# Head norms of a DeltaNet block through one shared root and a spreading product

## The chip, the cores and the metric

The kernel runs on one core of a Trainium2 chip. The metric is the device time of one execution in microseconds (us); lower is better. The engines are named as the profile names them: PE is TensorE (PEld its weight loads), ACT is ScalarE, DVE is VectorE, POOL is GpSimd and SP is SyncE, whose queue (SPq) issues the transfers.

## The reference

One decoder block, float32, 512 positions, width 1024. Its input projection feeds two token mixers, a gated DeltaNet and an RWKV-7 mixer, which are merged, projected, and followed by a ConvGLU. The change touches the start of the DeltaNet, which has 8 heads of 64 channels:

```python
def l2_normalize(x, eps=1e-6):
    return x * lax.rsqrt(jnp.sum(x * x, axis=-1, keepdims=True) + eps)

q = l2_normalize(heads(q)) * (GDN_HEAD_DIM ** -0.5)
k = l2_normalize(heads(k))
g = -jnp.exp(a_log) * jax.nn.softplus(a_logit + dt_bias)
...
diff = g_cum[..., :, None] - g_cum[..., None, :]
decay = jnp.where(causal, jnp.exp(jnp.where(causal, diff, 0.0)), 0.0)
lower = jnp.where(strict, einsum('bhncd,bhnsd->bhncs', k_beta, k) * decay, 0.0)
attn = jnp.where(causal, einsum('bhncd,bhnsd->bhncs', q, k) * decay, 0.0)
```

So each position's 64 channels of a head are divided by the root of their sum of squares (q and k), decay factors are made from the running sums of g in chunks of 64 positions, and the scores of k with k and of q with k are multiplied by them. A triangular solve per chunk and head follows.

## The kernel before

Activations lie with channels on the 128 partitions and the 512 positions along the free dimension. The DeltaNet's k and q are `kq[:, a, j]`, with a = 0 for k and a = 1 for q, and j = 0 to 3: eight tiles of 128x512, each holding two heads.

**The stream.** The large products (projections, FFN) are done in three TensorE products per 128 rows (`mm3`, lines 186, 189 and 190): the upper part of the weights by the upper part of the data, by its lower part, and the lower part of the weights by the upper part of the data. Weights come from memory to `raw` (line 156, issued by SP), and ACT casts them to `whi` (line 145), and DVE subtracts (line 148, `wlo`); each of these has two buffers. `fill(n)` puts n such steps of three products into the instruction stream between other work. The products of a tile of 128 outputs (8 steps, 24 products) go to a bank of `ps_mm`, of which there are two; the bank is read by ACT and DVE (lines 392, 394, 398, 399), or copied to `tmp_sp` and stored (lines 404, 405). The stream's tiles at this place in the program are, in order: one whose output is called LO1, then LO2, four Z tiles (stored by line 405) and four GV tiles.

**The norms.** `l2norm` (lines 486 to 493) is called eight times with two fills behind each: ACT squares the tile (line 488), PE multiplies by `ones_bd`, a block matrix of ones that puts each head's sum on all 64 of its partitions (line 490, an fp32 product 128*128 by 128x512 into a bank of `ps_pa`), ACT takes the logarithm and the exponential of minus a half of it (`rstd_of`, both recorded at line 94, output `tmp_rs`), and DVE multiplies (line 493).

**The decay parts.** A loop over b = 0 to 3 (lines 508 to 528) has one DVE product (line 510, `tmp_acc`), an fp32 product with `tri_gt` (line 514), an exponential on ACT into `tmp_sg`, two masks on POOL (line 519), a DVE product (line 521), then an fp32 product with `ones_x` (line 525), which sums over the 64 partitions of the other half, and an exponential into `eg`.

**The scores.** A loop over eight chunks (lines 627 to 635) has eight products of 64*64 by 64x128 (line 631) into one of three `ps_pa` banks, which DVE reads in three products (lines 632, 635, 635). A DVE product of 64x2048 (line 626) stands ahead of them in DVE's order. `solve` follows: SP writes the scores to memory in four transfers (line 556) and reads them back (line 559), then DVE runs a recursion of 30 steps (lines 567, 569).

**What sets the order.** The code is written in one order; a scheduler then sets each engine's instructions in a row of its own, and every engine works through its row in order. `ps_pa` has three banks, `ps_pc` has three, and `tmp_sq`, `tmp_rs`, `tmp_acc`, `tmp_sg` and `tmp_sp` have two buffers each.

Of the kernel before, what the change touches and what calls it, by code (L numbers as in the profile page):

```python
# [17 lines left out]
AF = mybir.ActivationFunctionType  # L18
ALU = mybir.AluOpType
# [23 lines left out]
CONS = {}  # L43
_n = 0
for _name, _w in (("ident", 128), ("tri_gt", 128), ("cumtri", 128),
                  ("ones_x", 128), ("mask2", 128), ("tri_le", 64), ("sel", 16)):
    CONS[_name] = (_n, _w)
    _n += _w
NCONS = _n
# [6 lines left out]
def body(ctx, tc, io, out, tap=lambda name, ap: None):  # L56
    nc = tc.nc
    pe, act, dve, pool, sp = nc.tensor, nc.scalar, nc.vector, nc.gpsimd, nc.sync
# [19 lines left out]
    pa = lambda: bank("pa", 3)  # L78
    pc = lambda: bank("pc", 3)
# [21 lines left out]
    def tmp(tag, bufs=2):  # L101
        return tp.tile([128, 512], F32, name=f"tmp_{tag}", tag=tag, bufs=bufs)
# [18 lines left out]
    def con(name):  # L121
        o, w = CONS[name]
        return cons[:, o:o + w]

    ident, tri_gt, cumtri = (con(n) for n in ("ident", "tri_gt", "cumtri"))
    mask2 = con("mask2").rearrange("p (a t) -> p a t", a=2)
    tri_le, sel, ones_x = con("tri_le"), con("sel"), con("ones_x")
    kc = const.tile([128, 4], F32, name="kc")
    for j, v in enumerate((EPS, LNX)):
        pool.memset(kc[:, j:j + 1], v)  # L130
# [143 lines left out]
    def fill(n=1):  # L274
        for _ in range(n):
            if gen[0] is None:
                if not queue:
                    return
                gen[0] = stream()
            try:  # L280
                next(gen[0])
            except StopIteration:
                gen[0] = None
# [10 lines left out]
    def rstd_of(p, scale, dst, bias=eps):  # L294
        fn(dst, p, AF.Ln, bias=bias, scale=scale)
        return fn(dst, dst, AF.Exp, scale=-0.5)
# [54 lines left out]
    p = pa()  # L351
# [131 lines left out]
    last["gate"] = dve.scalar_tensor_tensor(gl, s3, -1.0, bc(nea), op0=ALU.mult, op1=ALU.mult)  # L483


    def l2norm(dst, scale):
        sq = tmp("sq")
        act.activation(sq, dst, AF.Square)
        q = pa()
        pe.matmul(q, ones_bd, sq, start=True, stop=True)  # L490
        rs = tmp("rs")
        rstd_of(q, 1.0, rs)
        dve.scalar_tensor_tensor(dst, dst, scale, rs, op0=ALU.mult, op1=ALU.mult)

    eg = ct4(slot(3))
    ee = slot2(1)[:, 0:2048].rearrange("p (c h t) -> p c h t", c=NC, h=4)
    for j in range(4):
        l2norm(kq[:, 0, j], 1.0)
        fill(2)
        l2norm(kq[:, 1, j], 0.125)  # L500
        fill(2)
    p = pa()
    kdec = const.tile([128, NC, 4], F32, name="kdec")
    pe.matmul(p[:, 0:32], tri_gt, gl.rearrange("p c h -> p (c h)"), start=True, stop=True)
# [1 line left out]
    dve.tensor_tensor(kdec, kdec, beta, op=ALU.mult)  # L506

    for b in range(4):
        gt = tmp("acc").rearrange("p (c h t) -> p c h t", c=2, h=4)
        dve.tensor_tensor(gt, gl[:, 2 * b:2 * b + 2, :].unsqueeze(3).broadcast_to([128, 2, 4, C]),  # L510
                           tri_le.unsqueeze(1).unsqueeze(1).broadcast_to([128, 2, 4, C]), op=ALU.mult)
        gtf = gt.rearrange("p c h t -> p (c h t)")
        p = pa()
        pe.matmul(p, tri_gt, gtf, start=True, stop=True)
        ex = tmp("sg").rearrange("p (c h t) -> p c h t", c=2, h=4)
        fn(ex, p.rearrange("p (c h t) -> p c h t", c=2, h=4), AF.Exp)
        for e in range(2):
            d = ex[64 * e:64 * e + 64]
            pool.affine_select(out=d, in_=d, pattern=[[0, 2], [0, 4], [1, C]], base=0, channel_multiplier=-1,
                               compare_op=ALU.is_ge, fill=0.0)  # L520
        dve.tensor_tensor(ee[:, 2 * b:2 * b + 2], ex,
                          beta[:, 2 * b:2 * b + 2, :].unsqueeze(3).broadcast_to([128, 2, 4, C]), op=ALU.mult)
        fill(1)
        p = pa()
        pe.matmul(p, ones_x, gtf, start=True, stop=True)
        fn(eg[:, :, 128 * b:128 * b + 128].rearrange("p h (c t) -> p c h t", c=2),
           p.rearrange("p (c h t) -> p c h t", c=2, h=4), AF.Exp)
        fill(1)
# [98 lines left out]
    for c in range(NC):  # L627
        tc_ = slice(c * C, (c + 1) * C)
        p = pa().rearrange("p (h a t) -> p h a t", h=4, a=2)
        for ct, e, r in heads():  # L630
            pe.matmul(p[hs(1 - e), ct], ke[r, ct, tc_], kq[r, :, ct, tc_], start=True, stop=True)
        dve.tensor_tensor(ginv[:, c], p[:, :, 0], ee[:, c], op=ALU.mult)
        for e in range(2):
            q = hs(1 - e)
            dve.tensor_tensor(qs[e][q, :, tc_], p[q, :, 1], ee[q, c], op=ALU.mult)
    egl = const.tile([128, 4, NC], F32, name="egl")
    gsolve = solve(gs[:, 0:2048].rearrange("p (i t) -> p i t", i=32), "g", 10)
    next(gsolve)
# [447 lines left out]
def _arrays(inputs):  # L1086
    import numpy as np
    f = {k: np.asarray(v) for k, v in inputs.items()}
    tiled = lambda w: np.ascontiguousarray(
        w.reshape(w.shape[0] // 128, 128, w.shape[1] // 128, 128).transpose(2, 1, 0, 3)).reshape(  # L1090
            w.shape[1] // 128, 128, -1)
    percol = lambda v: v.reshape(-1, 128).T
    w_in = f["w_in"][0]
    z = lambda n: np.zeros((D, n), np.float32)
    q0, z0, b0, a0, r0 = 0, 1536, 2048, 2056, 2064
    k0, v0, wl, al, gl, ga, gb = r0 + 512, r0 + 1024, r0 + 1536, r0 + 1600, r0 + 1664, 3888, 4912
    perm = np.concatenate([
        w_in[:, gl + 128:gl + 160], w_in[:, b0:b0 + 8], w_in[:, a0:a0 + 8], z(80),
        w_in[:, q0 + 512:q0 + 1024], w_in[:, q0:q0 + 512], w_in[:, q0 + 1024:q0 + 1536],
        w_in[:, wl:wl + 128], w_in[:, gl:gl + 128],  # L1100
        w_in[:, k0:k0 + 512], w_in[:, r0:r0 + 512], w_in[:, v0:v0 + 512],
        w_in[:, z0:z0 + 512], w_in[:, ga:ga + 1024], w_in[:, gb:gb + 1024]], axis=1)
    w_fi = f["w_ffn_in"][0]
    w_fi = np.stack([w_fi[:, :DFF].reshape(D, NF, 128), w_fi[:, DFF:].reshape(D, NF, 128)], axis=2).reshape(D, 2 * DFF)
    w_fo = tiled(f["w_ffn_out"][0])
    mu = f["mu_rwkv"][0]
    rep = lambda v: np.repeat(v.reshape(4, 2).T[::-1], 64, axis=0)
    parts = {
        "norm1": percol(f["norm1_w"][0]), "norm2": percol(f["norm2_w"][0]), "normf": percol(f["norm_f_w"]),
        "conv_gdn": f["conv_gdn"][0].reshape(4, 12, 128).transpose(2, 1, 0).reshape(128, 48),  # L1110
        "mu": percol(mu[:1536]),
        "mu_lo": np.stack([mu[1536:1664], mu[1664:1792], np.concatenate([mu[1792:1824], np.zeros(96, np.float32)])], 1),
        "a0": percol(f["a0"][0]), "k_k": percol(f["k_k"][0]), "k_a": percol(f["k_a"][0]),
        "r_k": percol(f["r_k"][0].reshape(-1)), "lnx_w": percol(f["lnx_w"][0]), "lnx_b": percol(f["lnx_b"][0]),
        "conv_ffn": f["conv_ffn"][0].reshape(3, NF, 128).transpose(2, 1, 0).reshape(128, 3 * NF),
        "onorm": np.concatenate([f["onorm_gdn"][0], f["onorm_gdn"][0]])[:, None],
        "a_log": rep(f["a_log"][0]), "dt_bias": rep(f["dt_bias"][0]), "b_ada": percol(f["b_ada"][0])}
    i = np.arange(128)
    same = (i[:, None] // 64) == (i[None, :] // 64)
    s64 = np.arange(64)  # L1120
    sel = np.zeros((128, 16), np.float32)
    for e in range(2):
        for ct in range(4):
            sel[32 + 2 * ct + e, 8 * e + ct] = 1
            sel[40 + 2 * ct + e, 8 * e + 4 + ct] = 1
    le = np.tile((s64[:, None] <= s64[None, :]).astype(np.float32), (2, 1))
    lt = np.tile((s64[:, None] < s64[None, :]).astype(np.float32), (2, 1))
    cp = {"ident": np.eye(128),
          "tri_gt": same & (i[:, None] > i[None, :]),
          "cumtri": np.where(same & (i[:, None] <= i[None, :]), -math.exp(-0.5), 0.0),  # L1130
          "ones_x": ~same,
        "mask2": np.concatenate([lt, le], 1), "tri_le": le, "sel": sel}
    return {
        "xT": np.ascontiguousarray(f["x"][0].T.reshape(8, 128, T)),
        "c": np.broadcast_to(f["c"], (128, D)),
        "cols": np.concatenate([parts[n] for n in COLS], axis=1),
        "cons": np.concatenate([cp[n].astype(np.float32) for n in CONS], axis=1),
        "w_ada": np.ascontiguousarray(f["w_ada"][0].T.reshape(48, 128, D)),
        "w_in": tiled(perm), "w_bg": tiled(f["w_branch_gdn"][0]), "w_br": tiled(f["w_branch_rwkv"][0]),
        "w_out": tiled(f["w_out"][0]), "w_fi": tiled(w_fi), "w_fo": w_fo,  # L1140
        "w2": np.concatenate([f["w2"][0], f["w0"][0][None]], axis=0), "a2": f["a2"][0], "g2": f["g2"][0]}
# [23 lines left out]
```

## Time and profile before

| | |
|---|---|
| device time, three runs | 939.75 us median (938.65 to 940.68) |
| the profiled execution | 938.37 us, its span 936.4 us |
| mean granted TensorE clock | 0.98 |
| PE busy | 878.2 us, 94% of the span |
| DVE, ACT, POOL busy | 532.2, 424.3, 107.3 us |
| the chain that ended last, PE's share | 70% |

A row of the timeline gives the start and the duration in us, the engine, the line in the kernel, the operation, output and input, and in brackets how long the engine had stood idle and what it waited for. In a product's row, 128*128 is the weight's shape and 128x512 that of the moving data. An fp32 product stands in the trace as two matmuls (x2). Matmuls overlap, so what a product costs PE is read from the distance between starts, not from its duration. The stage that the change touches lies between 70 and 145 us from the start of the span.

### The profile page before, as it was taken

The page shows a single profiled execution, that of the slowest core. Times are in us where ns is not written, and L with a number is a line of the kernel's source. Part 1 is how long each engine was busy: PE and PEld are TensorE (multiplying, and loading weights), DVE is VectorE, ACT ScalarE, POOL GpSimd, SP SyncE. Part 2 cuts the span into 40 slices and gives each one's busy share as a digit, 9 for nine tenths or more (in the row PEclk, how much of TensorE's full clock was granted, in tenths as well). Part 3 has the DMA queues.
Part 4 walks back from the last instruction along what each step waited for, and adds up shares of the span by engine and source line. Part 5 has one row for each costly group of instructions (what it writes and reads, how often), then busy time and mean ns, then how long its engine had stood idle before and what let it go on. Part 6 is the DMA issues. An engine that isn't in the chain of part 4 may idle for free.

```text
span 936.4 us, 13900 instructions
## 1 busy us (share of the span) xinstructions
PE 878.2 (94%) x5459; PEld 687.0 (73%) x5459; DVE 532.2 (57%) x850; ACT 424.3 (45%) x691; POOL 107.3 (11%) x99
## 2 busy tenths in 40 slices
PE   2999989999999988999998999999999999999996
PEld 1886577676666666777665788888888888888885
DVE  5987859724796777245378537465444445332233
ACT  5368443734654838622466435343333333232231
POOL 1000310000361300001233320000000000010112
PEclk9999999998999989899999999999999999999998
DMA  9841254454233366744537542322332332533322
GB/s 340 284 161 57 79 138 158 130 138 137 89 91 100 86 219 225 185 143 159 176 120 255 178 153 83 106 97 90 100 103 90 96 108 90 176 100 101 101 85 90
DMA packets 81695, 126.77 MB, mean 135 GB/s; under 512 B 26109, under 2 KB 42877, under 8 KB 81566
## 3 DMA queue, kind: packets, MB, share of 16 engines
q1 hardware_dynamic: 81630, 125.88, 42.4%
q8 instruction: 43, 0.70, 0.3%
q14 instruction: 22, 0.18, 0.1%
HBM read 110.66 MB, written 14.68 MB: 134 GB/s over the span
## 4 chain that ended last, share of the span: by engine, by line
PE 70%; DVE 10%; ACT 8%; issue 6%; DMA 3%; POOL 2%; SPq 0%; DVEq 0%; ACTq 0%; POOLq 0%
PE ps_mm L186 19%; PE ps_mm L189 18%; PE ps_mm L190 18%; PE ps_pc L181 3%; DVE wlo L148 2%; ACT slot L615 2%; ACT tmp_rs L94 1%; PE ps_pc L186 1%; PE ps_pc L189 1%; PE ps_pc L190 1%; PE ps_pa L186 1%; ACT whi L145 1%; PE ps_pa L189 1%; PE ps_pa L190 1%; PE ps_pa L600 1%
## 5 line engine op out<-in xcount | busy, mean ns | idle before, releaser
L186 PE MATMUL ps_mm<-hh,whi 128*128 128x512 f32 (+1 forms) x714 | 291.2, 409 | 7.6 <-ACT hh L304 3.4
L190 PE MATMUL ps_mm<-hh,wlo 128*128 128x512 f32 (+1 forms) x714 | 280.8, 395 | 2.2 <-DVE wlo L148 2.2
L189 PE MATMUL ps_mm<-hl,whi 128*128 128x512 f32 (+1 forms) x714 | 280.8, 394 | 0.0
L148 DVE TENSOR_TENSOR wlo<-raw,whi 128x1024 fp32r<-128x1024 f32 (+2 forms) x140 | 161.1, 1151 | 184.5 <-ACT whi L145 178.2
L145 ACT CAST whi<-raw 128x1024 fp32r<-128x1024 f32 (+2 forms) x140 | 137.1, 979 | 246.5 <-PE ps_mm L189 188.0
L186 PEld LDWEIGHTS ps_mm<-hh,whi 128*128 128x128 f32 x714 | 135.4, 190 | 47.0 <-issue 7.0
L190 PEld LDWEIGHTS ps_mm<-hh,wlo 128*128 128x128 f32 x714 | 135.5, 190 | 34.2 <-DVE wlo L148 4.0
L189 PEld LDWEIGHTS ps_mm<-hl,whi 128*128 128x128 f32 x714 | 135.8, 190 | 29.9 <-issue 4.8
L186 PE MATMUL ps_mm<-slot,whi 128*128 128x512 f32 (+1 forms) x154 | 59.1, 385 | 2.7 <-ACT hh L145 1.5
L190 PE MATMUL ps_mm<-slot,wlo 128*128 128x512 f32 (+1 forms) x154 | 59.5, 386 | 1.8 <-DVE wlo L148 1.8
L189 PE MATMUL ps_mm<-slot,whi 128*128 128x512 f32 (+1 forms) x122 | 45.5, 373 | 0.2 <-DVE slot L148 0.2
L209 DVE CUSTOM_DVE_ANT_0 wada<-wada,cond,cols 128x512 f32<-128x512 f32 x32 | 25.0, 782 | 33.5 <-DMA wada<-in_w_ada 33.5
L190 PEld LDWEIGHTS ps_mm<-slot,wlo 128*128 128x128 f32 x154 | 29.7, 193 | 9.3 <-DVE wlo L148 4.2
L186 PEld LDWEIGHTS ps_mm<-slot,whi 128*128 128x128 f32 x154 | 29.7, 193 | 9.3 <-ACT hh L145 1.9
L186 PE MATMUL ps_mm<-slotd,whi 128*128 128x512 f32 (+1 forms) x96 | 36.4, 380 | 0.0
L190 PE MATMUL ps_mm<-slotd,wlo 128*128 128x512 f32 (+1 forms) x96 | 36.1, 376 | 0.0
L189 PE MATMUL ps_mm<-slotd,whi 128*128 128x512 f32 (+1 forms) x96 | 36.1, 376 | 0.0
L1040 DVE TENSOR_TENSOR tmp_sg<-tmp_acc,ps_mm 128x512 f32<-128x512 f32 x20 | 13.8, 688 | 35.6 <-PE ps_mm L190 35.5
L394 DVE SCALAR_TENSOR_TENSOR tmp_acc<-ps_mm,cols,tmp_acc 128x511 f32<-128x511 f32 (+2 forms) x44 | 32.8, 746 | 0.7
L973 POOL COPY tmp_rs<-tmp_sq 128x512 f32<-128x512 f32 x2 | 2.1, 1068 | 267.4 <-ACT tmp_sq L970 267.4
L94 ACT ACTIVATE tmp_acc<-tmp_acc 128x512 f32<-128x512 f32 x22 | 13.9, 631 | 41.5 <-DVE tmp_acc L394 41.4
L975 POOL TENSOR_TENSOR tmp_rs<-tmp_rs,tmp_sq 128x512 f32<-128x512 f32 x12 | 19.5, 1623 | 103.8 <-ACT tmp_sq L970 103.8
(266 smaller groups left out, 1286.7 us busy)
## 6 DMA issues: line engine op xcount, KB each, us to landing
raw<-in_w_in SPq DMA_DIRECT2D x40, 512.0 KB, 4.0
raw<-in_w_fi SPq DMA_DIRECT2D x37, 512.0 KB, 3.5
wada<-in_w_ada SPq DMA_DIRECT2D x64, 256.0 KB, 2.9
raw<-in_w_fo SPq DMA_DIRECT2D x16, 512.0 KB, 3.5
slot<-in_w_ada SPq DMA_DIRECT2D x10, 512.0 KB, 8.5
slot<-in_xT SPq DMA_DIRECT2D x16, 256.0 KB, 4.2
raw<-in_w_out SPq DMA_DIRECT2D x8, 512.0 KB, 3.6
raw<-in_w_in SPq DMA_DIRECT2D x8, 448.0 KB, 4.5
```

The lines of the kernel that those rows point to most:

```text
L94: i = act.activation(*a, **k)
L145: i = act.copy(hi, src)
L148: j = eng.tensor_tensor(lo, src, hi.bitcast(F32), op=ALU.subtract)
L181: last["step"] = pe.matmul(*a, **k)
L186: i = pe.matmul(p, hi, xh, start=start, stop=False)
L189: pe.matmul(p, hi, xl, start=False, stop=False)
L190: pe.matmul(p, lo, xh, start=False, stop=stop)
L209: i = dve.tensor_tensor_reduce(out=w, in0=w, in1=cond[:, part], scale=1.0, scalar=half[:, j:j + 1] if u else col("b_ada", j), op0=ALU.mult ...
L394: dve.scalar_tensor_tensor(acc[:, i:], p[:, :T - i], w[:, taps - 1 - i:taps - i], acc[:, i:], op0=ALU.mult, op1=ALU.add)
L615: (act.copy if e == c or quiet else dve.tensor_copy)(place(e, 2 * b + c), p[hs(c), :, e, :])
L975: pool.tensor_tensor(sums[0], sums[0], sq, op=ALU.add)
L1040: dve.tensor_tensor(t, accs[j], p, op=ALU.mult)
```

## The change

The eight norms are no longer done one by one. For each of k and q, the four tiles are squared, and each square is multiplied by 32 columns of the block of ones (`head_sum`: 16 columns for one head and 16 for the other), so that the sums of the four tiles land on the four groups of 32 partitions of one bank. One logarithm and one exponential of 128x512 then serve four tiles. To get a tile's factors back to 128 partitions, an fp32 product with a new constant `spread` (weights 32*128) writes them to a bank of `ps_pc` or `ps_pa`, and DVE multiplies from there. These spreads (`normed`) are put into the decay loop, two tiles in each of its four passes. `ones_x` goes: in its place are two products with a 64x64 block of ones. There are four fills in place of sixteen in the norms, eight in `normed`, and one more behind each chunk of the scores. In the changed kernel lines lie one further down at the start and 12 to 16 further down behind the norms.

```diff
-    def l2norm(dst, scale):
-        sq = tmp("sq")
-        act.activation(sq, dst, AF.Square)
-        q = pa()
-        pe.matmul(q, ones_bd, sq, start=True, stop=True)
-        rs = tmp("rs")
-        rstd_of(q, 1.0, rs)
-        dve.scalar_tensor_tensor(dst, dst, scale, rs, op0=ALU.mult, op1=ALU.mult)
+    head_sum = ones_bd[:, 48:80]
+
+    def over_channels(rs, ks):
+        banks = [(pa if k % 2 else pc)() for k in ks]
+        for k, b in zip(ks, banks):
+            pe.matmul(b, spread[32 * k:32 * k + 32], rs[32 * k:32 * k + 32], start=True, stop=True)
+        return banks
...
-    for j in range(4):
-        l2norm(kq[:, 0, j], 1.0)
+    norms = [tmp("rs") for _ in range(2)]
+    for a in range(2):
+        q = pa()
+        for j in range(4):
+            sq = tmp("sq")
+            act.activation(sq, kq[:, a, j], AF.Square)
+            pe.matmul(q[32 * j:32 * j + 32], head_sum, sq, start=True, stop=True)
+        rstd_of(q, 1.0, norms[a])
         fill(2)
-        l2norm(kq[:, 1, j], 0.125)
+
+    def normed(a, ks):
+        for k, b in zip(ks, over_channels(norms[a], ks)):
+            dve.scalar_tensor_tensor(kq[:, a, k], kq[:, a, k], (1.0, 0.125)[a], b, op0=ALU.mult, op1=ALU.mult)
         fill(2)
...
     for b in range(4):
+        normed(b // 2, (2 * (b % 2), 2 * (b % 2) + 1))
...
-        pe.matmul(p, ones_x, gtf, start=True, stop=True)
+        for e in range(2):
+            pe.matmul(p[64 - 64 * e:128 - 64 * e], one[64 * e:64 * e + 64, 0:64], gtf[64 * e:64 * e + 64],
+                      start=True, stop=True)
...
             dve.tensor_tensor(qs[e][q, :, tc_], p[q, :, 1], ee[q, c], op=ALU.mult)
+        fill(1)
...
+          "spread": (i[:, None] % 32 == 0) & same[0:1] | (i[:, None] % 32 == 16) & ~same[0:1]}
```

Three places in the rows of the engines show it. The first is PE's row in the decay loop. Before, L514 and L525 are the two products of a pass, and L186, L189 and L190 are the stream:

```order
L514 MATMUL ps_pa<-tmp_acc,cons 128x512
L186 MATMUL ps_mm<-hh_107,whi 128x512
L189 MATMUL ps_mm<-hl_115,whi 128x512
L190 MATMUL ps_mm<-hh_107,wlo 128x512
L186 MATMUL ps_mm<-hh_108,whi 128x512
L525 MATMUL ps_pa<-tmp_acc,cons 128x512
L514 MATMUL ps_pa<-tmp_acc,cons 128x512
L525 MATMUL ps_pa<-tmp_acc,cons 128x512
L189 MATMUL ps_mm<-hl_116,whi 128x512
```

The same place now, where L527 is the product with `tri_gt`, L539 the pair of 64x64 products, L494 a spread, and L187, L190 and L191 the stream:

```order
L187 MATMUL ps_mm<-hh_105,whi 128x512
L527 MATMUL ps_pa<-tmp_acc,cons 128x512
L539 MATMUL ps_pa<-tmp_acc,one 64x512 x2
L494 MATMUL ps_pa<-tmp_rs,cons 128x512
L527 MATMUL ps_pa<-tmp_acc,cons 128x512
L539 MATMUL ps_pa<-tmp_acc,one 64x512 x2
L494 MATMUL ps_pa<-tmp_rs,cons 128x512
L527 MATMUL ps_pa<-tmp_acc,cons 128x512
L539 MATMUL ps_pa<-tmp_acc,one 64x512 x2
L494 MATMUL ps_pa<-tmp_rs,cons 128x512
L190 MATMUL ps_mm<-hl_113,whi 128x512
```

Spreads stand between the decay products, and no product of the stream does so for three passes. Ahead of that place the other four spreads stand in `ps_pc`, and the eight head sums (L505) stand in runs of two, one, three, one and one, the last two with spreads ahead of each.

The second place is PE's row in the scores. Before, where L631 are the score products, 24 of them stand together, and between the next eights there is one product of the stream:

```order
L631 MATMUL ps_pa<-slotd_459 64x128 x24
L186 MATMUL ps_mm<-hh_104,whi 128x512
L189 MATMUL ps_mm<-hl_112,whi 128x512
L190 MATMUL ps_mm<-hh_104,wlo 128x512
L631 MATMUL ps_pa<-slotd_459 64x128 x8
L186 MATMUL ps_mm<-hh_105,whi 128x512
L631 MATMUL ps_pa<-slotd_459 64x128 x8
L189 MATMUL ps_mm<-hl_113,whi 128x512
L631 MATMUL ps_pa<-slotd_459 64x128 x8
L190 MATMUL ps_mm<-hh_105,wlo 128x512
L631 MATMUL ps_pa<-slotd_459 64x128 x16
```

Now, where L646 are the score products, each eight has three products of the stream behind it, eight times over:

```order
L646 MATMUL ps_pa<-slotd_459 64x128 x8
L187 MATMUL ps_mm<-hh_108,whi 128x512
L190 MATMUL ps_mm<-hl_116,whi 128x512
L191 MATMUL ps_mm<-hh_108,wlo 128x512
L646 MATMUL ps_pa<-slotd_459 64x128 x8
L187 MATMUL ps_mm<-hh_109,whi 128x512
```

The third place is SP's row, from the first weights behind the constants to the solve. `raw` are weights, `zsc` the stored Z tiles, `lsc_g` the scores on their way to the solve. Before:

```order
L156 DMA raw<-in_w_in 128x1024 x6
L208 DMA wada<-in_w_ada 128x512 x2
L156 DMA raw<-in_w_in 128x1024
L208 DMA wada<-in_w_ada 128x512 x3
L405 DMA zsc<-tmp_sp 128x512
L556 DMA lsc_g<-slotd_851 32x32x32 x4
L405 DMA zsc<-tmp_sp 128x512 x2
L156 DMA raw<-in_w_in 128x1024
L559 DMA slot_957<-lsc_g 128x1024
```

And now:

```order
L157 DMA raw<-in_w_in 128x1024 x7
L209 DMA wada<-in_w_ada 128x512 x3
L406 DMA zsc<-tmp_sp 128x512
L209 DMA wada<-in_w_ada 128x512
L157 DMA raw<-in_w_in 128x1024
L571 DMA lsc_g<-slotd_832 32x32x32 x4
L406 DMA zsc<-tmp_sp 128x512 x2
L157 DMA raw<-in_w_in 128x1024
L574 DMA slot_972<-lsc_g 128x1024
```

The weights of the first GV tile (the ninth `raw` behind the constants; one stands just ahead of these rows) stood behind the scores' transfers and two stored Z tiles; they now stand ahead of both.

More of the change, by code (lines that the diff above doesn't have):

```diff
@@ L45 @@
 for _name, _w in (("ident", 128), ("tri_gt", 128), ("cumtri", 128),
-                  ("ones_x", 128), ("mask2", 128), ("tri_le", 64), ("sel", 16)):
+                  ("mask2", 128), ("tri_le", 64), ("sel", 16), ("spread", 128)):
     CONS[_name] = (_n, _w)
@@ L126, in body @@
     mask2 = con("mask2").rearrange("p (a t) -> p a t", a=2)
-    tri_le, sel, ones_x = con("tri_le"), con("sel"), con("ones_x")
+    spread = con("spread")
+    tri_le, sel = con("tri_le"), con("sel")
     kc = const.tile([128, 4], F32, name="kc")
@@ L1130, in _arrays @@
           "cumtri": np.where(same & (i[:, None] <= i[None, :]), -math.exp(-0.5), 0.0),
-          "ones_x": ~same,
-        "mask2": np.concatenate([lt, le], 1), "tri_le": le, "sel": sel}
+        "mask2": np.concatenate([lt, le], 1), "tri_le": le, "sel": sel,
+          "spread": (i[:, None] % 32 == 0) & same[0:1] | (i[:, None] % 32 == 16) & ~same[0:1]}
     return {
```

## The prediction

> **What bounds the kernel now.** I read the page's first part and its chain of waits first.
>
> ```profile
> PE 878.2 (94%) x5459; PEld 687.0 (73%) x5459; DVE 532.2 (57%) x850; ACT 424.3 (45%) x691; POOL 107.3 (11%) x99
> PE 70%; DVE 10%; ACT 8%; issue 6%; DMA 3%; POOL 2%; SPq 0%; DVEq 0%; ACTq 0%; POOLq 0%
> ```
>
> PE is busy for 94% of the span. The stream's products all have to be done, wherever the fills put them. So a fill that moves costs nothing, and the time changes by the work that PE gets or loses, by the waits in its row, and by its clock. Next are the waits of PE between 60 and 145 us (sum, times, longest):
>
> ```profile
> PE ps_mm L186 <- DVE tmp_acc L394: 2.1, 1, 2.1
> PE ps_mm L186 <- ACT whi L145: 1.7, 1, 1.7
> PE ps_pa L514 <- DVE tmp_acc L510: 1.2, 1, 1.2
> PE ps_pa L631 <- DVE slotd L635: 1.0, 1, 1.0
> PE ps_mm L190 <- DVE wlo L148: 0.5, 1, 0.5
> PE ps_pa L612 <- ACT slot L615: 0.2, 1, 0.2
> ```
>
> Then the table by stretches: length, busy time of PE, PEld, DVE, ACT and POOL, granted clock, DMA.
>
> ```profile
> 80.45:84.20 3.75, 3.75 (x10) 2.94 (x11) 1.39 (x5) 3.73 (x9) 0.00 (x0) 0.54 0.39 140
> 84.20:96.00 11.80, 11.80 (x42) 7.41 (x41) 9.46 (x24) 10.65 (x20) 0.00 (x0) 1.00 0.15 45
> 138.40:142.20 3.80, 3.80 (x10) 2.98 (x11) 2.24 (x7) 1.04 (x1) 1.27 (x1) 0.55 0.86 315
> ```
>
> The norms lie between 84 and 96. ACT is busy there for 10.65 of 11.80 us, but PE for all of it: ACT's load is hidden by the stream. Behind the two longest waits the clock is about half.
>
> **What goes.** Six logarithms and six exponentials leave ACT. They lie in the stretch in which PE never waits, so I cost them at nothing; the eight products of DVE stay.
>
> The six waits are 6.7 us. Each is counted from a modelled end:
>
> ```profile
> 88.12 0.40 PE L186 MATMUL ps_mm<-hh,whi 128*128 128x512 f32 x1
> 88.36 0.40 PE L189 MATMUL ps_mm<-hl,whi 128*128 128x512 f32 x1
> 88.59 1.02 PE L490 MATMUL ps_pa<-tmp_sq,ones_r 128*128 128x512 f32 x2
> 89.05 0.79 PE L190 MATMUL ps_mm<-hh,wlo 128*128 128x512 f32 x1
> 89.68 0.39 PE L186 MATMUL ps_mm<-hh,whi 128*128 128x512 f32 x1
> ```
>
> A product of the stream is shown for 0.39 but steps by 0.23, so the row loses 0.16 more each time: 6.7 + 6 x 0.16 = 7.7 us. From 88.59 to 89.68 lie one L490 and one L190: an fp32 product of 512 columns costs 1.09 - 0.23 = 0.86.
>
> Why they go. The wait of 2.1 is for a `ps_mm` bank: DVE had a weight split of 1.23 us ahead of the bank's last reader, and in the new row that split stands behind it. The 1.2 was L510 queued on DVE behind a product that waited for POOL; there is a spread between the passes now. The 1.0 was DVE's three reads against 24 score products at once; now three products of the stream stand behind each eight. The 1.7 and 0.5 are the first GV tile's weights:
>
> ```profile
> 94.92 0.33 SPq L156 DMA_DIRECT2D raw<-in_w_in  x1
> 97.56 9.48 SPq L208 DMA_DIRECT2D wada<-in_w_ada  x3
> 108.40 0.33 SPq L405 DMA_DIRECT2D zsc<-tmp_sp  x1
> 119.14 3.51 SPq L556 DMA_DIRECT2D lsc_g<-slotd  x4
> 126.59 4.45 SPq L405 DMA_DIRECT2D zsc<-tmp_sp  x2
> 131.57 0.33 SPq L156 DMA_DIRECT2D raw<-in_w_in  x1
> ```
>
> The transfer left at 131.57, behind two stores of Z tiles that wait for ACT's copies, and PE ran dry at 135.3. In the new SP row it stands ahead of the scores' four transfers, and no longer behind the stores.
>
> The two half-speed stretches follow the waits of 2.1 and 1.7; without them I expect no drop. They cost 3.75 x 0.46 + 3.80 x 0.45 = 3.4 us. [...]
>
> Together 7.7 + 3.4 = 11.1 us go.
>
> **What comes.** Eight spreads, weights 32*128. The trace has such a product, L930:
>
> ```profile
> 473.73 0.50 PE L175 MATMUL ps_pa<-tmp_sp,ones_r 128*128 128x512 f32 x1
> 474.16 1.12 PE L930 MATMUL ps_pa<-sg,slotd 32*128 32x512 f32 x2
> 475.21 0.50 PE L174 MATMUL ps_pa<-tmp_sg,ones_r 128*128 128x512 f32 x1
> 475.55 0.39 PE L175 MATMUL ps_pa<-tmp_sp,ones_r 128*128 128x512 f32 x1
> 473.73 0.19 PEld L175 LDWEIGHTS ps_pa<-tmp_sp,ones_r 128*128 128x128 f32 x1 [0.82 <-POOL tmp_sp L148]
> 474.16 0.29 PEld L930 LDWEIGHTS ps_pa<-sg,slotd 32*128 32x128 f32 x2 [0.24 <-issue]
> ```
>
> A quarter of the rows saves nothing: it takes 1.05 where the full shape takes 0.86. So eight spreads cost 8 x 0.86 = 6.9 us, plus the change of shape, which the rows price: 0.19 in L930 itself, whose weights load only when it starts; 0.11 on the follower, which steps by 0.34; and about 0.10 ahead (L175 steps by 0.43, of which its own late weights are 0.11). That is 0.40 for a stretch of another shape inside the stream. Between two narrow shapes I take 0.20, by this L695 behind 64*64 products:
>
> ```profile
> 232.29 1.12 PE L695 MATMUL ps_pa<-slot 64*128 64x512 f32 x2
> 233.34 0.50 PE L186 MATMUL ps_mm<-hh,whi 128*128 128x512 f32 x1
> 233.68 0.40 PE L189 MATMUL ps_mm<-hl,whi 128*128 128x512 f32 x1
> ```
>
> The new row has 11 such stretches (three of head sums alone, one mixed, three single spreads, three pairs L539 each with a spread, one pair) and 6 inner changes: 11 x 0.40 + 6 x 0.20 = 5.6 us. Before, all products here were full. In the scores there are eight narrow stretches for five:
>
> ```profile
> 113.17 1.09 PE L631 MATMUL ps_pa<-slotd 64*64 64x128 f32 x16
> 114.19 0.50 PE L189 MATMUL ps_mm<-hl,whi 128*128 128x512 f32 x1
> 114.62 1.09 PE L631 MATMUL ps_pa<-slotd 64*64 64x128 f32 x16
> 116.07 1.96 PE L631 MATMUL ps_pa<-slotd 64*64 64x128 f32 x32
> 117.97 0.50 PE L186 MATMUL ps_mm<-hh,whi 128*128 128x512 f32 x1
> ```
>
> Sixteen score products take 1.90, eight with one product of the stream 1.45: 1.45 - 0.95 - 0.23 = 0.27 a stretch, 0.8 for three. Shape changes: 6.4 us. Bounds: nothing, if at 512 columns the loads hide as in the full shape; 0.51 a stretch, if L175's whole delay counts, 1.2 more.
>
> The pairs L539 lie on different halves of the array, as the score products of a chunk do. One of those is 128 columns wide, which alone would be 0.86 / 4 = 0.22; sixteen in 1.90 take 0.12 each, so two run at once. I let each pair cost 0.86, as one full product does; at worst it is 1.72 (a rival). Head sums share the rows of the array but not the columns; these two starts show such products together:
>
> ```profile
> 398.35 0.27 PE L181 MATMUL ps_pc<-slot,slotd 128*64 128x64 f32 x1
> 398.36 0.27 PE L181 MATMUL ps_pc<-slotd,slot 128*64 128x64 f32 x1
> ```
>
> So the run of two and the first two of the run of three save 0.86 each: 1.7 us. The third of that run waits for its square, since `tmp_sq` has two buffers and the square starts when the first sum is done: about 0.7 us of a wait (a square is 0.62 long):
>
> ```profile
> 87.43 0.62 ACT L488 ACTIVATE tmp_sq<-slotd 128x512 f32<-128x512 f32 x1
> ```
>
> Behind it in PE's row is LO2, whose bank is free by then. [...]
>
> The added fills are moved, not added. DVE reads the spreads from PSUM; it has 2.3 us of slack in the stretch above.
>
> **The sum.** 6.9 + 6.4 - 1.7 + 0.7 - 11.1 = +1.2 us. The profiled execution took 938.37, its span 936.4; with the change 939.6. It lies 1.38 below the median of the runs, so against 939.75 I say 941.0. A measurement can tell about 0.2%, 1.9 us, so this is within it. With the shape bound of 1.2 it is 2.4, just outside.
>
> **Rivals.**
>
> Products do not overlap at 512 columns. For: the trace has only 64 and 128 columns in such pairs, where the second's weights load in a gap. It decides at the pairs L539 and the runs of head sums: 4 x 0.86 + (1.7 - 0.7) = +4.4, 945.4, slower. Against: the pairs at 398.35 start together. 0.14.
>
> The shape changes cost nothing at this width. Place: the 11 stretches; -5.6, 935.4, faster. It decides when a stretch costs under 0.2. Against: L930 and L695 are 512 wide and show it. 0.14, with partial forms.
>
> The weights' wait stays, because the buffer that the transfer needs is freed late (a DVE split in the middle of the scores frees it) or the cast stands behind another wait: 1.7 + 0.5 + 0.3 and the clock's 1.7 come back, +4.2, 945.2. 0.12.
>
> [...]
>
> The lighter ACT also removes a later wait. Between 168 and 182 PE is busy for 12.49 of 14.00 us while ACT copies:
>
> ```profile
> 168.00:182.00 14.00, 12.49 (x47) 7.40 (x46) 12.18 (x36) 13.55 (x28) 0.00 (x0) 1.00 0.25 76
> ```
>
> That would give 1.5 back, 939.5. Against: that work starts behind the solve, not behind the norms. 0.10.
>
> **The numbers.** The forecast, 941.0, has 0.42, with its own range 939.0 to 943.5. Faster by over 0.2%: 0.14 and 0.03 of the forecast and of the last rival each, 0.20. Within 0.2%: 0.24 of the forecast and 0.07, 0.31. Slower: 0.15 of the forecast, 0.14, 0.12 and 0.08, 0.49. The range that leaves out under 0.2 runs from 937.0 (half of the shape rival) to 945.6 (past the first and third rival).
>
> **What would show it.** L494 stepping by 1.05 or so, L539 x2 by 0.86 to 1.1, L187 behind a narrow product by 0.34. PE's waits from 60 to 145 us near 1 instead of 6.7, with the clock at 1.00. The transfer of the first GV weights ahead of the scores' four. Wrong it is if a pair L539 takes 1.7, if PE still runs dry near 140, or if the clock falls between 96 and 110.

## The result, and the profile after

The changed kernel takes 946.2 us (median of 11 runs, 940.9 to 947.7); the kernel before took 938.7 in the runs beside it. The ratio is 1.0064, 95% interval 1.0045 to 1.0083: 6.0 us slower, between 4.2 and 7.8. The forecast was 1.2 us more than before, 941.0, and the median lies 0.6 above the upper end of its range; the same ratio on the 939.75 of the forecast gives 945.8, 0.2 above that end. The sign was the one that I had given 0.49, and the size was wrong.

The profiled execution of the changed kernel has a span of 944.7 us, 8.3 more than before. The page's first part and its chain of waits, of the kernel after:

```profile
PE 891.6 (94%) x5483; PEld 686.5 (73%) x5483; DVE 532.1 (56%) x850; ACT 419.3 (44%) x679; POOL 107.5 (11%) x99
PE 72%; DVE 10%; ACT 5%; DMA 5%; issue 5%; POOL 2%; SPq 0%; DVEq 0%; ACTq 0%; POOLq 0%
```

PE is busy for 13.4 us more. ACT lost 5 us of work, and nothing came of it. The waits of PE between 60 and 150 us, where six stood before, after:

```profile
PE ps_pa L505 <- ACT tmp_sq L504: 0.7, 1, 0.7
```

Only the wait for the third square is left, at the length that I gave it. So the waits did go. The starts of PE's products, after, price what came (L505 are head sums, L494 spreads, L527 and L539 the decay products):

```profile
72.39 1.05 PE L505 MATMUL ps_pa<-tmp_sq,ones_r 128*32 128x512 f32 x4
73.37 0.50 PE L187 MATMUL ps_mm<-hh,whi 128*128 128x512 f32 x1
...
92.07 1.12 PE L494 MATMUL ps_pc<-tmp_rs,cons 32*128 32x512 f32 x2
93.12 0.51 PE L191 MATMUL ps_mm<-hh,wlo 128*128 128x512 f32 x1
...
94.94 1.37 PE L494 MATMUL ps_pa<-tmp_rs,cons 32*128 32x512 f32 x2
96.24 0.80 PE L187 MATMUL ps_mm<-hh,whi 128*128 128x512 f32 x1
96.83 0.63 PE L190 MATMUL ps_mm<-hl,whi 128*128 128x512 f32 x1
...
99.56 1.08 PE L539 MATMUL ps_pa<-tmp_acc,one 64*64 64x512 f32 x4
100.56 1.12 PE L494 MATMUL ps_pa<-tmp_rs,cons 32*128 32x512 f32 x2
101.61 1.12 PE L527 MATMUL ps_pa<-tmp_acc,cons 128*128 128x512 f32 x2
```

Two head sums together take 0.98, a pair L539 takes 1.00, a spread 1.05: all near the prices of the prediction. But from 94.94 on a spread takes 1.30 and a product of the stream steps by 0.43, with no wait ahead of it. The table by stretches (columns as in the prediction), after:

```profile
92.28:95.69 3.41, 3.41 (x9) 1.15 (x8) 2.34 (x5) 1.82 (x3) 0.00 (x0) 1.00 0.44 154
95.69:99.10 3.41, 3.41 (x7) 1.83 (x6) 2.92 (x5) 0.00 (x0) 0.00 (x0) 0.50 0.52 154
138.40:142.20 3.80, 3.80 (x19) 3.14 (x18) 1.05 (x1) 0.27 (x1) 0.00 (x0) 1.00 0.49 169
222.00:235.60 13.60, 13.60 (x132) 8.51 (x126) 4.84 (x8) 7.78 (x14) 0.62 (x1) 0.50 0.36 118
```

The two half-speed stretches of before are gone, that near 140 among them. But PE is busy for the whole of 92.28 to 95.69, and at 95.69 the clock halves. It is also half for 13.6 us behind the first solve, where it had been so for 10.3. This row of before answers to the last one:

```profile
206.90:217.20 10.30, 10.30 (x162) 7.56 (x163) 3.82 (x6) 6.30 (x10) 0.00 (x0) 0.50 0.33 85
```

To see where the 8.3 us come from I cut both executions at the same products and took 0.227 off for each product of the stream in a stage, since the fills moved between the stages. The norms and decay parts run from the last product at L454 (L455 after) to the first score product. The middle columns come from starts and counts of PE's rows.

| stage | before | after | difference | forecast |
|---|---|---|---|---|
| up to 71 us | | | +0.6 | 0 |
| norms and decay: length, products of the stream | 36.17, 72 | 40.59, 60 | | |
| the same without the stream | 19.8 | 27.0 | +7.1 | +6.2 |
| scores without the stream | 9.5 | 9.5 | 0.0 | -0.4 |
| scores to the end of the first 64 of the solve's products L590 or L605, without the stream | 16.9 | 12.3 | -4.6 | -4.6 |
| from there to the product that stood at 231 us | | | +1.6 | 0 |
| behind it | | | +3.6 | 0 |

The sum is 8.3. The forecast column splits the prediction's terms by place and adds up to its +1.2. In the norms the forecast is off by 0.9 only, because two errors cancel: the half speed that came, 3.41 x 0.5 = 1.7, and 0.8 less for everything else. Most of the rest of the difference lies behind the solve, where I had expected nothing.

### The profile page after: what moved, and what is told of

The parts are those of the page before. It is cut to its first block, busy times and chain, and to the rows that moved or that the text cites. A ratio compares the mean times of both kernels' runs of the same rounds, so it can differ in the third digit from the quotient of the medians.

```text
span 944.7 us, 13930 instructions
## 1 busy us (share of the span) xinstructions
PE 891.6 (94%) x5483; PEld 686.5 (73%) x5483; DVE 532.1 (56%) x850; ACT 419.3 (44%) x679; POOL 107.5 (11%) x99
## 4 chain that ended last, share of the span: by engine, by line
PE 72%; DVE 10%; ACT 5%; DMA 5%; issue 5%; POOL 2%; SPq 0%; DVEq 0%; ACTq 0%; POOLq 0%
PE ps_mm L187 19%; PE ps_mm L190 18%; PE ps_mm L191 18%; PE ps_pc L182 3%; DMA wada<-in_w_ada 2%; DVE wlo L149 2%; DVE wada L210 1%; PE ps_pc L187 1%; PE ps_pc L190 1%; PE ps_pc L191 1%; PE ps_pa L190 1%; PE ps_pa L187 1%; PE ps_pa L191 1%; ACT whi L146 1%; PE ps_pa L646 1%
## 5 line engine op out<-in xcount | busy, mean ns | idle before, releaser
L187 PE MATMUL ps_mm<-hh,whi 128*128 128x512 f32 (+1 forms) x714 | 290.4, 407 | 3.4 <-ACT hh L305 3.4
L191 PE MATMUL ps_mm<-hh,wlo 128*128 128x512 f32 (+1 forms) x714 | 278.8, 392 | 1.9 <-DVE wlo L149 1.9
L190 PE MATMUL ps_mm<-hl,whi 128*128 128x512 f32 (+1 forms) x714 | 279.2, 391 | 0.0
L187 PEld LDWEIGHTS ps_mm<-hh,whi 128*128 128x128 f32 x714 | 135.2, 190 | 46.3 <-issue 11.8
L191 PEld LDWEIGHTS ps_mm<-hh,wlo 128*128 128x128 f32 x714 | 135.3, 190 | 32.6 <-DVE wlo L149 3.2
L190 PEld LDWEIGHTS ps_mm<-hl,whi 128*128 128x128 f32 x714 | 135.6, 190 | 28.7 <-issue 4.0
L187 PE MATMUL ps_mm<-slot,whi 128*128 128x512 f32 (+1 forms) x154 | 60.1, 390 | 2.9 <-ACT whi L146 1.7
L191 PE MATMUL ps_mm<-slot,wlo 128*128 128x512 f32 (+1 forms) x154 | 60.4, 392 | 1.3 <-DVE wlo L149 1.3
L190 PE MATMUL ps_mm<-slot,whi 128*128 128x512 f32 (+1 forms) x122 | 46.0, 377 | 0.0
L187 PEld LDWEIGHTS ps_mm<-slot,whi 128*128 128x128 f32 x154 | 30.1, 196 | 10.4 <-ACT whi L146 3.8
L191 PEld LDWEIGHTS ps_mm<-slot,wlo 128*128 128x128 f32 x154 | 30.0, 195 | 8.9 <-DVE wlo L149 3.6
L187 PE MATMUL ps_mm<-slotd,whi 128*128 128x512 f32 (+1 forms) x96 | 36.4, 380 | 0.0
L191 PE MATMUL ps_mm<-slotd,wlo 128*128 128x512 f32 (+1 forms) x96 | 36.1, 376 | 0.0
L190 PE MATMUL ps_mm<-slotd,whi 128*128 128x512 f32 (+1 forms) x96 | 36.1, 376 | 0.0
```

The source lines that it names most:

```text
L187: i = pe.matmul(p, hi, xh, start=start, stop=False)
L190: pe.matmul(p, hi, xl, start=False, stop=False)
L191: pe.matmul(p, lo, xh, start=False, stop=stop)
```

## The experiments

Every ratio is against the kernel before, run beside it on the same chip.

**The changed kernel once more.**

> The changed kernel once more, for a second trace of it. Theory A (the clock): what my sum of +1.2 us lacks is half-speed clock. In the first trace it fell for one stretch of 3.4 us at 95.7, in a run of narrow products without any wait of PE (1.7 us lost), and lasted one stretch longer behind the first solve, because 49 products of the stream that stood behind the solve now stand ahead of it (1.9 us); the two later differences (a second solve's half speed one stretch longer, 1.7, and a stall near 516 with its own half-speed stretch, 1.5) are chance. Then this trace has the half speed again behind the first solve for four stretches (13.7 us) and once between 85 and 108 us, while the later two may be missing; time 943 to 948. Theory B (prices): narrow products and changes of shape cost more than I counted, and the clock has little part in it. Then the starts between 70 and 128 us show more than my prices, and the time is the same 946 whether the half-speed stretches are there or not.

Measured: 945.7 us, ratio 1.0070 (1.0048 to 1.0092). Two rows of the table by stretches of this run:

```profile
95.10:101.90 6.80, 6.80 (x13) 2.51 (x12) 3.49 (x7) 0.80 (x2) 0.41 (x1) 0.50 0.24 77
224.80:231.60 6.80, 6.66 (x49) 3.86 (x51) 4.00 (x6) 4.88 (x9) 0.00 (x0) 0.50 0.32 116
```

The half speed in the narrow products is back, and twice as long: the norms and decay parts cost 28.6 here, 8.8 more than before. Behind the solve it lasts 6.8 us, less than before the change. So the first half of theory A holds, and its second half does not hold in every execution.

**Without the fill behind each chunk of the scores.**

```diff
             dve.tensor_tensor(qs[e][q, :, tc_], p[q, :, 1], ee[q, c], op=ALU.mult)
-        fill(1)
```

> The changed kernel without the fill behind each chunk of the scores. In its row 49 products of the stream stand behind the solve again, as before the change; but the first GV weights are again queued behind the scores' four transfers. Theory A: the half speed behind the solve lasts 10.2 us instead of 13.7, and 1.9 us come back; three narrow stretches fewer give 0.8; the scores' wait returns with 1.0: 944.5. If PE runs dry for the GV weights again (2.2 of waits, 0.3 of overlap, 1.7 of clock), 948.7. Theory B: the place of the solve is worth nothing: 946.4, or 950.6 with the weights' wait.

Measured: 947.2 us, ratio 1.0088 (1.0073 to 1.0103). PE's waits between 120 and 160 us:

```profile
PE ps_mm L187 <- ACT whi L146: 1.7, 1, 1.7
PE ps_mm L191 <- DVE wlo L149: 1.1, 2, 0.5
PE ps_pa L627 <- ACT slot L630: 0.2, 1, 0.2
```

PE runs dry for the GV weights again, with its half-speed stretch (at 147.5), and the half speed behind the solve is 10.2 us. Theory A's 948.7 is 1.5 off, theory B's 950.6 is 3.4 off. The norms and decay parts cost 27.0, as in the changed kernel.

**Only that fill.**

```diff
             dve.tensor_tensor(qs[e][q, :, tc_], p[q, :, 1], ee[q, c], op=ALU.mult)
+        fill(1)
```

> The kernel before with the added fill behind each chunk of the scores and nothing else. Its row for SP has the first GV weights ahead of the scores' transfers, and 25 products of the stream stand behind the solve instead of 49. By the sum of the prediction the scores' wait (1.0), the weights' two waits (2.2 and 0.3 of overlap) and their half-speed stretch (1.7) go, and three narrow stretches come (0.8): 938.7 - 5.2 + 0.8 = 934.3. Theory A: the same, or up to 1.9 more if 25 products are too few for the clock to recover on, 936.2. Rival: the waits only move (PE runs dry elsewhere), 938.7 or more.

Measured: 941.8 us, ratio 1.0029 (1.0015 to 1.0042), slower, where both numbers of the expectation were faster. PE's waits between 60 and 150 us:

```profile
PE ps_mm L186 <- DVE tmp_acc L394: 2.1, 1, 2.1
PE ps_mm L186 <- ACT whi L145: 1.7, 1, 1.7
PE ps_pa L612 <- ACT slot L94: 1.4, 1, 1.4
...
```

The scores' 1.0 went, and a wait of 1.4 came at 144.9. The 1.7 looks like that of before, but it belongs to other weights. ACT's casts in this run:

```profile
130.00 1.05 ACT L145 CAST whi<-raw 128x1024 fp32r<-128x1024 f32 x1 [0.28 <-PE ps_mm L189]
...
141.69 1.03 ACT L145 CAST whi<-raw 128x1024 fp32r<-128x1024 f32 x1
```

The weights of the first GV tile now leave at 112.78, ahead of the scores' transfers, are cast at 130.00, and PE starts on them at 135.47 without a wait. The wait is that of the second GV tile, whose weights leave at 136.76, behind two stored Z tiles, and are cast at 141.69. The rival is right: the waits moved. Neither wait is there when the fill and the new norms come together.

**Every product of the norms and decay parts in the full shape.** The four block matrices lie in a free slot.

```diff
...
-            pe.matmul(b, spread[32 * k:32 * k + 32], rs[32 * k:32 * k + 32], start=True, stop=True)
+            pe.matmul(b, spread4[:, 128 * k:128 * k + 128], rs, start=True, stop=True)
...
-            pe.matmul(q[32 * j:32 * j + 32], head_sum, sq, start=True, stop=True)
+            pe.matmul(q, sums4[:, 128 * j:128 * j + 128], sq, start=j == 0, stop=j == 3)
...
-        for e in range(2):
-            pe.matmul(p[64 - 64 * e:128 - 64 * e], one[64 * e:64 * e + 64, 0:64], gtf[64 * e:64 * e + 64],
-                      start=True, stop=True)
+        pe.matmul(p, ones_x, gtf, start=True, stop=True)
```

> The changed kernel with every product of its norms and of its decay parts in the full shape 128*128: the head sums by four block matrices that add up in one bank, the spreads by weights that are zero outside their 32 rows, and one product with off-diagonal ones in place of the pair. The results are the same; the block matrices are made by POOL early on. The array works fully in every product, and no shape changes there. Theory A: no half speed between 85 and 108; it stays behind the solve for four stretches. From before: 8 spreads x 0.86 = 6.9, scores 0.8, less 11.1 of waits and clock, plus 1.9 behind the solve: 938.7 - 1.5 = 937.2. Theory B: the narrow products were the whole excess: 938.7 + 6.9 + 0.8 - 11.1 = 935.3. If shape and clock mattered little, it stays near 946.

Measured: 941.3 us, ratio 1.0026 (1.0017 to 1.0036): 4.4 us less than the changed kernel beside it. The stretch of the norms and decay parts, and that behind the solve:

```profile
71.70:107.60 35.90, 35.46 (x119) 20.36 (x116) 26.84 (x51) 19.92 (x37) 6.42 (x8) 1.00 0.18 59
218.80:232.50 13.70, 13.70 (x105) 8.27 (x98) 5.03 (x8) 7.00 (x13) 0.62 (x1) 0.50 0.37 117
```

The clock is 1.00 throughout the first, and half for 13.7 us behind the solve, as theory A has it. The norms and decay parts cost 22.3, against 27.0 and 28.6. The time is 4.1 over theory A's number; 2.7 of that lies behind 231 us.

**The disputed cost by itself.** Twelve extra products in a row, put into the kernel before behind the scores; the shape is the only thing that changes between the three runs (`0:64` and `0:128` stand in place of `0:32` in the others). Their results are not used.

```diff
+    p = pc()
+    for _ in range(12):
+        pe.matmul(p, ident[0:32], qe[0:32, 0], start=True, stop=True)
     need(T_GV + 3)
```

> The kernel before with twelve extra fp32 products 32*128 by 32x512 in a row, behind the scores and ahead of the solve, whose results are not used. No wait belongs to them. They fill PE while it waits for the first GV weights, so up to 4.2 us of that come back. Theory A (the clock follows how much of the array works): a product of 32 rows that takes 1.05 us where the full shape takes 0.86 works the array by 0.25 x 0.86 / 1.05 = 0.20, about what the stretches ahead of the half speed in the first traces have; so after one stretch of 3.4 us in the run the clock halves, with PE busy all the time, and the rest of the run, seven or eight products, steps by 2.0: the time is 7 to 10 us over that of the same run with 64 rows. Theory B (only waits and idle time halve the clock): products step by 1.05 to the end, and the time is that of the run with 64 rows, 938.9 + 13.0 - 4.2 = 947.7.

> The same twelve extra products with 64 rows, 64*128 by 64x512. Theory A: the array works by 0.5 x 0.86 / 1.05 = 0.41, more than ahead of any half speed in the traces, so the clock stays at 1.00 and each product steps by 1.05: 938.9 + 12 x 1.05 + 0.4 - 4.2 = 947.7. Theory B: the same 947.7.

> The same twelve extra products in the full shape, 128*128 by 128x512. Both theories: 0.86 each, no change of shape, clock 1.00: 938.9 + 10.3 - 4.2 = 945.0. Against the run with 64 rows it prices the shape by itself: 12 x 0.19 + 0.4 = 2.7 less, or nothing if the price of a quarter of the rows lies elsewhere.

Measured: with 32 rows 959.3 us, ratio 1.0214 (1.0197 to 1.0231); with 64 rows 951.3, 1.0127 (1.0108 to 1.0147); with 128 rows 949.6, 1.0111 (1.0096 to 1.0126). The run of twelve and what follows it, with 32 rows:

```profile
125.56 15.96 PE L647 MATMUL ps_pc<-slotd,cons 32*128 32x512 f32 x24
141.45 0.79 PE L186 MATMUL ps_mm<-hh,whi 128*128 128x512 f32 x1
```

With 64 rows:

```profile
126.03 0.39 PE L190 MATMUL ps_mm<-hh,wlo 128*128 128x512 f32 x1
126.35 10.56 PE L647 MATMUL ps_pc<-slotd,cons 64*128 64x512 f32 x24
136.84 0.50 PE L186 MATMUL ps_mm<-hh,whi 128*128 128x512 f32 x1
137.18 0.40 PE L189 MATMUL ps_mm<-hl,whi 128*128 128x512 f32 x1
```

With 128 rows:

```profile
125.68 0.40 PE L190 MATMUL ps_mm<-hh,wlo 128*128 128x512 f32 x1
125.91 10.46 PE L647 MATMUL ps_pc<-slotd,cons 128*128 128x512 f32 x24
135.81 0.79 PE L186 MATMUL ps_mm<-hh,whi 128*128 128x512 f32 x1
136.44 0.40 PE L189 MATMUL ps_mm<-hl,whi 128*128 128x512 f32 x1
```

Here are the steps of the twelve products, from their starts:

```
32 rows:  0.96 0.86 0.86 0.86 0.86 1.12 1.71 1.71 1.71 1.71 1.71 1.84
64 rows:  0.96 0.86 0.86 0.86 0.86 0.86 0.86 0.86 0.86 0.86 0.86 0.95
```

And two rows of the table by stretches, first with 32 rows and then with 64:

```profile
127.10:130.50 3.40, 3.40 (x10) 1.45 (x9) 1.83 (x3) 0.51 (x1) 0.00 (x0) 1.00 0.61 127
130.50:144.10 13.60, 13.60 (x20) 5.83 (x19) 2.70 (x8) 0.00 (x0) 1.27 (x1) 0.50 0.34 123
```

```profile
127.10:130.50 3.40, 3.40 (x9) 1.49 (x8) 2.39 (x4) 1.29 (x2) 0.00 (x0) 1.00 0.38 96
130.50:144.10 13.60, 13.60 (x47) 8.42 (x47) 3.32 (x9) 1.53 (x2) 1.27 (x1) 1.00 0.36 132
```

With 32 rows PE never waits, and after one stretch of 3.4 us that holds 32-row products alone the clock halves and stays half until the run is over. With 64 rows it stays at 1.00. The difference of the two times is 8.0 us, within the 7 to 10 of theory A; theory B had none. Second, inside a run a narrow product costs what a full one does, 0.86; only the change of shape costs. From the last product ahead to the second one behind, 64 rows take 137.18 - 126.03 = 11.15 us and 128 rows 136.44 - 125.68 = 10.76: 0.39 for the one stretch, where the prediction had 0.40. The runs with 64 and 128 rows are 3.6 and 4.6 us longer than I expected, the first although its products step by 0.19 less than I had put in. The shape is not the reason, since both have it; the cause stays open.

**The kernel before once more.**

> The kernel before once more, for a second trace. In all four later traces the part behind 231 us is longer than in the first trace of before by 1.7 to 3.6 us, though the products are the same. If that is chance of the first trace, this one has more half-speed stretches or waits behind 231 us than the first (six and a half stretches there), and its early part is faster than the first's by as much. If it is the ripple of the change (products of the stream that stand at other places around 330 to 520 us), this trace agrees with the first of before behind 231 us within 1 us.

Measured: 939.1 us, ratio 1.0003 (0.9991 to 1.0015). This trace lies 0.9 behind the first at 231 us and 1.3 at the end, so 0.5 comes behind 231: they agree. But the three runs with twelve products, whose norms are those of before, lose 3.0, 2.6 and 1.4 there. So a part of the +3.6 may be owed to any change ahead of it. One piece belongs to the changed rows: between the stream's products that stood at 478.07 and 484.08 us all seven traces with new norms or the added fill lose 0.7 to 1.5, and the other six nothing. In the changed kernel PE waits 0.5 for POOL there; the two that lose more than 0.8 have a half-speed stretch that begins there. What decides the rest stays open.

**Only the spreads in the full shape** (the first hunk of the full-shape kernel alone), **and only the product with ones** (its last hunk alone).

> The changed kernel with only the spreads in the full shape (weights 128*128 that are zero outside their 32 rows); head sums and pairs stay narrow. The run of twelve products showed that 32 rows cost the same 0.86 inside a run, and that they take the clock down. Theory A: it is the spreads, each with a quarter of the array, that halve the clock near 95; with them full no half speed lies between 85 and 108 (1.7 to 3.4 back), and some seven stretches of another shape fewer give 0.2 each, 1.4: 945.9 - 2.5 - 1.4 = 942. If head sums and pairs were to blame as well, the half speed stays and only 1.4 comes back: 944.5.

> The changed kernel with only the pair of 64*64 products replaced by one full product with off-diagonal ones; the spreads stay at 32 rows. Theory A: the half speed near 95 stays, since the four spreads and two head sums ahead of the decay loop are what is narrow there; the four products cost 0.86 instead of 1.00: 945.9 - 0.6 = 945.3. If the pairs had their part in the clock, the half speed goes and 2 more come back: 943.

Measured: 943.5 us, ratio 1.0047 (1.0035 to 1.0060), and 946.2, 1.0081 (1.0060 to 1.0101). Full spreads, the norms and decay parts:

```profile
71.10:108.40 37.30, 36.59 (x128) 16.88 (x124) 26.04 (x48) 20.28 (x38) 6.02 (x9) 1.00 0.18 57
```

A full product with ones, the stretch behind the spreads:

```profile
94.90:101.70 6.80, 6.80 (x12) 3.04 (x11) 3.61 (x7) 0.79 (x2) 0.21 (x1) 0.50 0.24 77
```

It is the spreads that halve the clock. With them full the norms and decay parts cost 23.7; the 3.3 against the first trace of the changed kernel are 1.7 of clock and 1.6 of shapes. Theory A's numbers are 1.5 and 0.9 off. By the times alone the rival of the first, 944.5, would do as well; the clock decides it.

**The stores issued by ACT, in the kernel before; and the same with the norms inside the decay loop.**

```diff
             act.copy(o, p)
-            sp.dma_start(dst, o)
+            act.dma_start(dst, o)
```

```diff
-    for j in range(4):
-        l2norm(kq[:, 0, j], 1.0)
-        fill(2)
-        l2norm(kq[:, 1, j], 0.125)
-        fill(2)
+    fill(4)
...
     for b in range(4):
+        for k in (2 * (b % 2), 2 * (b % 2) + 1):
+            l2norm(kq[:, b // 2, k], (1.0, 0.125)[b // 2])
+            fill(1)
```

> The kernel before with one edit: the stored tiles (the Z tiles among them) are issued by ACT behind its own copy instead of by SP. The first GV weights then stand behind the scores' four transfers only, and leave near 123 instead of 131.6. By the prediction's price of that wait (1.7 + 0.5 of waits, 0.3 of overlap, 1.7 of half clock) this gives 938.9 - 4.2 = 934.7, without any narrow product. [...]

> The kernel before with its own eight norms (one full product each), two of them at the head of each pass of the decay loop, and the stores issued by ACT. PE gets no product more than before and none that is narrow. If the interleaving is what removes the waits of 2.1 and 1.2, and the first half-speed stretch with them, these give 3.6 + 1.7, and the stores 4.2: 938.9 - 9.5 = 929.4. Rival: the norms, now later in the row, wait for each other (a square, a logarithm and an exponential stand between a norm's product and the next use), so that PE's waits come back inside the decay loop: 935 to 939.

Measured: 938.8 us, ratio 0.9998 (0.9986 to 1.0010), and 939.9, 1.0007 (0.9995 to 1.0019): no change from either. With the stores on ACT, SP, ACT and PE around the GV weights (L404 is the copy of a Z tile, L145 the cast of the weights):

```profile
123.94 5.18 SPq L156 DMA_DIRECT2D raw<-in_w_in  x2
...
137.01 0.58 ACT L404 COPY tmp_sp<-ps_mm 128x512 f32<-128x512 f32 x1 [4.85 <-PE ps_mm L190]
...
138.05 2.00 ACT L145 CAST whi<-raw 128x1024 fp32r<-128x1024 f32 x2 [0.45 <-ACT tmp_sp L404]
...
139.15 0.50 PE L186 MATMUL ps_mm<-hh,whi 128*128 128x512 f32 x1 [2.17 <-ACT whi L145]
```

Both transfers have left by 129.1, and PE still waits 2.2: the cast stands in ACT's row behind the copy of the last Z tile, and that copy waits for PE's own product. The same two rows of ACT in the kernel before, and after:

```profile
135.52 0.59 ACT L404 COPY tmp_sp<-ps_mm 128x512 f32<-128x512 f32 x1 [4.85 <-PE ps_mm L190]
136.00 1.05 ACT L145 CAST whi<-raw 128x1024 fp32r<-128x1024 f32 x1
```

```profile
137.14 1.06 ACT L146 CAST whi<-raw 128x1024 fp32r<-128x1024 f32 x1 [1.69 <-PE ps_mm L190]
138.09 0.58 ACT L405 COPY tmp_sp<-ps_mm 128x512 f32<-128x512 f32 x1
```

In the changed kernel the cast stands ahead of the last two Z copies, and PE's first product with these weights comes at 142.61. With the norms in the decay loop the waits move there, as the rival had it; PE's waits between 60 and 110 us in that kernel:

```profile
PE ps_mm L186 <- DVE slot L399: 4.0, 1, 4.0
PE ps_pa L500 <- DVE gl L483: 0.5, 1, 0.5
```

No kernel of this study beats the one before.

## Where the prediction held and where it failed, point by point

**The number.** That the sign agrees is in part luck. Of the 0.49 for slower, 0.41 stood on the forecast's own tail and on two rivals that did not come, and the upper end of the range was set past those two. Only 0.08, for a half clock that comes without the waits, stood on what happened.

**The waits.** Right: from 6.7 us to 0.7, with the third square's wait as sized. The stage behind the scores gained the 4.6 that I had counted. The reason given for 2.2 of it, the late transfer, was at most half of it: with the transfer early the wait stays until the cast has another place in ACT's row. The run with the added fill alone agrees: there the first GV cast stands ahead of the last two Z copies too, and its wait is gone. I had read SP's queue and not ACT's.

**The prices.** Right: 0.40 a stretch was measured as 0.39, pairs and head sums overlap (0.98 to 1.00 for two), and the sum of these terms was 0.8 too high. That a product of 32 rows costs 1.05 was a change of shape on both sides, and not the product. The rivals of products that don't overlap, of shapes that cost nothing and of the weights' wait that stays are wrong.

**The clock.** Here the step failed: "The two half-speed stretches follow the waits of 2.1 and 1.7; without them I expect no drop." The clock was at half from 95.69 to 99.10 with no wait ahead of it; a fall between 96 and 110 was among the prediction's signs of being wrong. In these traces the half-speed stretches follow stretches in which the array did little work, and a wait is only one way to that: counted as in the last section, the stretches ahead of them hold 0.35 and 0.21 of the array's time before, 0.24 in the changed kernel and 0.25 in the run of twelve products of 32 rows. Nor does a wait suffice: with the stores on ACT the wait of 2.2 falls across the border of two stretches, which hold 0.66 and 0.45, and the clock stays at 1.00. I took the waits for the cause because they were the only case in the rows of before. The spreads are the other way: the run of twelve products shows it with PE busy all the time, and full spreads remove it. It costs 1.7 or 3.4 in an execution. Of my chances only the 0.08 allowed for this.

**The moved fills.** "The added fills are moved, not added" is true of their work, and I costed the move at nothing. In the changed row 48 products of the stream that stood behind the solve stand ahead of it. What follows the solve are narrow products, so the clock has little to recover on: in the changed kernel the half-speed stretches at 225.4 and 228.8 us hold 0.27 and 0.24 of the array's time and another follows each, where before the one at 213.8 holds 0.38 and is the last. With the 48 ahead, as in the changed kernel, the half speed there lasted 4, 2, 4, 5 and 5 stretches of 3.41 us in five traces (the changed kernel twice, the three with full shapes); with them behind, it lasted 3 in five of five (the kernel before twice, the changed one without the fill, and the two with the stores on ACT). With 24 ahead (the added fill alone) it lasted 3 as well, and with 48 more behind than before (the three runs of twelve products) 2, 3 and 3. Measured from the end of the solve's first 64 products to the product of 231 us, the first five differ from before by +1.6, -1.1, +1.9, +2.4 and +2.4, 1.4 on average. That is argued from traces that differ in other things too; no run moved these products alone.

**What is left.** For the profiled execution: 1.2 forecast, 1.7 for the clock in the norms, 0.8 less for the prices, 0.4 in the scores, 1.6 behind the solve, 0.6 ahead of 71 us, and 3.6 behind 231 us make 8.3. The 0.6 is chance: other traces have -0.1 to 1.8 there. The 3.6 is between 1.7 and 4.6 in the traces with new norms or the added fill, and between -2.9 and 3.0 in the others. In the profiled execution the clock can account for most of it: from 231 us to the last product of the stream the changed kernel's first trace has 20.5 us at half speed and that of before 13.7, and 6.8 us at half speed can cost 3.4. The extremes agree (24.9 us and +4.6 with the full product with ones, 6.8 us and -2.9 with the stores on ACT), but the second trace of before has 17.1 us and is only 0.5 longer. Why those stretches come is not settled. Which stretches fall where differs from one execution to the next, and so does the time: 941 to 948 us in eleven runs.

## What to carry to other kernels

When a product is narrowed to a part of the array, count two things: the change of shape, once for each stretch (0.39 us here), and the share of the array over the next few microseconds, since PE can be busy and still lose its clock (here after 3.4 us of 32-row products, 0.25 of the array). A full product took the same 0.86 us inside a run here, and with zero-padded spreads of the full shape the clock stayed at 1.00 in the norms and decay parts. Products that are moved ahead of a narrow stage may not be free even where PE never waits (argued here, not shown): ask what stands behind that stage for the clock to recover on. For a wait on a cast, read the row of the engine that casts before the queue that loads.

## What the runs showed of the hardware

In the clock records of the kernel before and of the changed one the half-speed stretches last 3.41, 6.83, 10.24 or 13.65 us, one to four times 3.41, but for the one in which the program ends. I divided the traces into stretches of 3.41 us from where the clock records begin (22.61 us before, 24.01 after), and gave each product its full-speed time on PE (for 512 columns 0.227 us in the stream and 0.86 for an fp32 product, in proportion for fewer) times its share of the 128x128 array. Counted so, the full-speed stretches that half speed followed, up to the first solve, hold these shares of the array's time: before 0.35 (from 77.22 us), 0.21 (135.25) and 0.05 (203.51), after 0.24 (92.28) and 0.07 (218.57). The one from 85.45 after holds 0.36, and the clock stayed at 1.00 behind it. Behind the first solve, at half speed, the stretches with 0.06 and 0.23 before and with 0.14, 0.27 and 0.24 after were followed by another; those with 0.38 before and 0.45 after were the last. That of 0.41 at 338.04 after was followed by another all the same. The twelve products of 32 rows gave 0.25 with PE busy, and the clock halved; those of 64 rows gave 0.50, and it stayed at 1.00. They narrow the rows alone; that columns count in the same way is an assumption of this count, and no run narrows them alone.

In the runs of twelve, products of 32 rows by 512 columns step by 0.86, as those of 128 rows do, and by 1.71 at half speed. In the changed kernel two fp32 products of 512 columns take 0.98 together on different column groups of the array (L505) and 1.00 on different halves (L539).
